# Two products with high and low values side by side, and probabilities scaled on another engine

## The chip, the cores and the metric

The kernel runs on one core of one Trainium2 chip. The metric is device time in microseconds (us) of one execution, the median of several runs. TensorE (PE in the profile) multiplies matrices, with weight loads shown as an engine of their own (PEld); VectorE is DVE, ScalarE is ACT, GpSimd is POOL, SyncE (SP) starts most DMA transfers. Each engine works through its own list of instructions strictly in order and waits at an instruction whose inputs or buffers are not ready.

## The reference, cut to what matters

One decoder layer over 1024 rows of width 1024: a token mixer, a cross-attention, a gated MLP. The change touches one head group of the mixer, sliding-window attention with 8 query heads that share 2 key and value heads of width 64, in blocks of 128 rows:

```
logits = einsum('bnqhgd,bnkhd->bnhgqk', qb, kb) * (SWA_HEAD_DIM ** -0.5)
logits = where(valid, logits + bias, -inf)
mx = maximum(logits.max(-1), sink)
p = exp(logits - mx)
probs = p / (p.sum(-1) + exp(sink - mx))
out = einsum('bnhgqk,bnkhd->bnqhgd', probs, vb)
```

Each block of 128 queries sees its own 128 keys and the 128 before them. Everything is in float32.

## The kernel before, in words

A float32 operand of a product is kept as two tiles, a rounded high part and the low part that is left (`hi_lo`: ScalarE copies, VectorE subtracts). A product is then three matmuls, `mm3`: high by high, high by low, low by high.

The mixer works through the sequence in two halves of 512 rows. In each half a generator, `swa`, walks through 16 items: 4 blocks of queries by 4 pairs of heads (`p`; its key and value head is `p // 2`). In the text items 0 to 15 are those of the first half, 16 to 31 those of the second. The generator hands its steps out between groups of matmuls of the projections, which are counted by an estimated clock (`tick`), so the place of each step in every engine's list is fixed when the program is built. Step *n* of `swa` issues, in this order: the logits of item *n* (`swa_logits`: four matmuls into a tile `lg`, then two custom VectorE instructions that write L and the row maxima `nm`), the values of item *n - 4* (`swa_values`, tile `pv`), the transposes of item *n - 2* (`swa_turn`, tile `tp`; ScalarE and VectorE make its two halves `pt`), the exponentials of item *n* (`swa_exp`, ScalarE, with the row sums `ssum`), and its scaling by the reciprocal of the sums (`swa_norm`). `lg`, `pv` and `tp` come from the pool `mx`, which has four PSUM banks; who gets which bank, and so who waits for whom, is decided when the program is built.

For most of items 1 to 11, and 17 to 27, the projections in between are the eight channel groups of `qk_proj`. Each has 24 matmuls of 512 columns, and a chain of its own (`qk_steps`): ScalarE copies the result (`xc`), GpSimd starts `cv`, VectorE adds three taps to `cv`, ScalarE takes a tanh (`th`), VectorE makes `qk` of it. In each group ScalarE and VectorE also split the weights that will be needed two groups on (`whi`, `wlo`).

`swv` holds the values: before, two tiles of 128 columns a block (both value heads), one with high and one with low parts. `swa_values` multiplies all 128 columns, though an item needs only the 64 of its own head:

```
mm3(pf, swv[0][:, cc, :], swv[1][:, cc, :], pt[0][:, m, :], pt[1][:, m, :], m == kb, m == 1)
r = slice(64 * (p // 2), 64 * (p // 2) + 64)
nc.scalar.copy(swT[h][p % 2][r, :, tt * P:(tt + 1) * P], pv[r])
```

`m` runs over the two blocks of keys; items 0 to 3 have one.

Of the kernel before, what the change touches and what calls it, by code (L numbers as in the profile page):

```python
# [7 lines left out]
F32 = mybir.dt.float32  # L8
F32R = mybir.dt.float32r
# [6 lines left out]
P = 128  # L16
# [12 lines left out]
def decoder_layer_kernel(ctx, tc, t, out):  # L29
    nc = tc.nc  # L30
    MUL, ADD, SUB, MAX, MIN = ALU.mult, ALU.add, ALU.subtract, ALU.max, ALU.min
# [47 lines left out]
    def hi_lo(hi, lo, src):  # L79
        nc.scalar.copy(hi, src)  # L80
        nc.vector.tensor_tensor(lo, in0=src, in1=hi.bitcast(F32), op=SUB)  # L81
# [63 lines left out]
    def mm3(ps, ahi, alo, bhi, blo, start, stop, more=False):  # L145
        nc.tensor.matmul(ps, lhsT=ahi, rhs=bhi, start=start, stop=False, skip_group_check=more)  # L146
        nc.tensor.matmul(ps, lhsT=ahi, rhs=blo, start=False, stop=False, skip_group_check=more)  # L147
        nc.tensor.matmul(ps, lhsT=alo, rhs=bhi, start=False, stop=stop, skip_group_check=more)  # L148
# [32 lines left out]
    def proj_tm(key, x, n, done, nt=4, before=None):  # L181
        pss = mm_tiles(nt)
        ws = {}
        us = 0.65 if n > 264 else 0.33
        a, b = range(0, nt // 2), range(nt // 2, nt)
        for j, tts in ((0, a), (1, a), (0, b), (1, b), (2, a), (2, b), (3, a), (3, b)):
            if before:
                before(j, tts is a)
            if j not in ws:
                ws[j] = weights(*key, j, ahead=2 if j != 1 else 0)  # L190
            elif (j, tts) == (1, b):
                stage(used[0] + 1)
            for tt in tts:
                for kk in range(2):
                    k, c = 2 * j + kk, slice(tt * P, (tt + 1) * P)
                    mm3(pss[tt][:, :n], x.hi(k, c), x.lo(k, c), ws[j][0][:, kk, :], ws[j][1][:, kk, :],
                        k == 0, k == KT - 1)
                    tick(us)
            if j == 3:
                for tt in tts:  # L200
                    done(tt, pss[tt])
# [65 lines left out]
    da = stA.enter_context(tc.tile_pool(name="da", bufs=1))  # L267
# [9 lines left out]

    kk = [da.tile([P, 5 * P], F32R, name=f"kk{i}") for i in range(2)]
    klo = [da.tile([P, 5 * P], F32R, name=f"klo{i}") for i in range(2)]
    swv = [da.tile([P, 5, P], F32R, name=f"swv{i}") for i in range(2)]  # L280
    halo = da.tile([P, 8, 3], F32, name="halo")
    gat = da.tile([P, 2, 4, 2, 16], F32, name="gat")
    mcol = da.tile([P, 3], F32, name="mcol")
# [4 lines left out]
    swT = [None, None]  # L288
# [40 lines left out]
    def ta_put(h, tt, ps):  # L329
        va = da.tile([P, 4, 129], F32, tag="va", name="va", bufs=5)  # L330
        nc.gpsimd.memset(va[:, :, 128:129], 1.0)
        va_t[4 * h + tt] = va
        nc.scalar.copy(va[:, 0, 0:128], ps[:, 0:128])
        hi_lo(swv[0][:, tt + 1, :], swv[1][:, tt + 1, :], ps[:, 128:256])
        for d in range(2):
            nc.vector.tensor_copy(gat[:, :, tt, d, 0:4], ps[:, 256:264].rearrange("p (a b) -> p a b", a=2))  # L336

    def tm_a(h, x):
        for z in swv:
            nc.vector.tensor_copy(z[:, 0, :], z[:, 4, :].bitcast(F32))  # L340
        proj_tm(("w_ta",), x, 264, lambda tt, ps: ta_put(h, tt, ps))

    def ta_first():
# [46 lines left out]
        for tt in range(4):  # L390
            ta_put(0, tt, pss[tt])
# [72 lines left out]
    def swa_norm(h, tt, p, kb, L, nm, sums):  # L464
        nc.vector.reciprocal(sums, sums)
        for b in range(2):
            Lv = L[:, b, kb * P:256]
            if b < 0:
                nc.scalar.mul(Lv, Lv, sums[:, b:b + 1])
            else:  # L470
                nc.vector.tensor_scalar(Lv, Lv, sums[:, b:b + 1], None, MUL)
        return h, tt, p, kb, L

    def swa_turn(h, tt, p, kb, L):
# [9 lines left out]
    def swa_values(h, tt, p, kb, pt):  # L484
        pv = mx.tile([P, 2, P], F32, tag="mx", name="pv")
        pf = pv.rearrange("p a b -> p (a b)")
        for m in range(kb, 2):
            cc = tt + m
            mm3(pf, swv[0][:, cc, :], swv[1][:, cc, :], pt[0][:, m, :], pt[1][:, m, :], m == kb, m == 1)
        r = slice(64 * (p // 2), 64 * (p // 2) + 64)  # L490
        nc.scalar.copy(swT[h][p % 2][r, :, tt * P:(tt + 1) * P], pv[r])

    def swa(h, swq, us):
        items = [(h, tt, p) for tt in range(4) for p in (0, 2, 1, 3)]
        lg, turned = [], []
        for n in range(len(items) + 4):
            if n < len(items):
                lg.append(swa_logits(*items[n], swq))
                yield 0.6
            if len(turned) == 2 or n == len(items) + 3:  # L500
                swa_values(*turned.pop(0))
                yield 0.6
            if n > 1 and lg:
                turned.append(swa_turn(*lg.pop(0)[:5]))
            if n >= len(items):
                yield us - 0.6
                continue
            yield 0.3
            swa_exp(*lg[-1])
            yield 0.65  # L510
            swa_norm(*lg[-1])
            yield us - (2.15 if n > 2 else 1.55)
# [224 lines left out]
    tm_o(1, x)  # L737
    drain()
    tm_a(1, x)
    also(gates(1, gt1, 2.7))  # L740
    s1 = also(swa(1, swq, 3.3), 1.0)
# [225 lines left out]
    vraw, graw, sums, pairs = {}, {}, {}, {}  # L967
# [281 lines left out]
    for h in range(2):  # L1249
# [5 lines left out]
        for tt in range(4):  # L1255
# [9 lines left out]
            if final:  # L1265
                for ch, b in ((1, 0), (0, None), (1, 1)):
                    v = slice(512 * ch, 512 * ch + 512) if b is None else slice(512 + 256 * b, 768 + 256 * b)
                    ps = banks[h, tt, ch][:, slice(0, 512) if b is None else slice(256 * b, 256 * b + 256)]
# [109 lines left out]
```

## Time and profile before

| | |
|---|---|
| median of 3 runs | 1415.21 us (1415.0 to 1415.45) |
| the profiled execution | 1416.47 us |
| its span, first to last instruction | 1414.8 us |
| PE busy | 1386.4 us, 98% |
| DVE busy | 973.1 us, 69% |
| ACT busy | 627.0 us, 44% |
| mean granted clock of TensorE | 0.995 |

The profile is of one execution, so its durations are set against 1416.47 us; 1.67 us of that lie outside the span. A busy share is a mean over the whole program: what bounds a stretch is read from the stretch.

### The profile page before, as it was taken

How to read it: one execution, taken by the hardware profiler on the slowest of the kernel's cores; microseconds unless marked ns; L12 is line 12 of the kernel's file. 1: busy time of each engine (PE TensorE's matmuls, PEld its weight loads, DVE VectorE, ACT ScalarE, POOL GpSimd, SP SyncE). 2: the span in 40 equal slices, each digit the busy share in tenths (PEclk: the TensorE clock that was granted, in tenths of full speed). 3: DMA queues.
4: the chain of work that ended last, by engine and by line, in shares of the span. 5: the costliest groups of instructions: out<-in, count | busy, mean ns of one | idle time of the engine just before them, and what ended most of it. 6: DMA issues, size and time to landing. Idle time of an engine off the chain costs nothing.

```text
span 1414.8 us, 18089 instructions
## 1 busy us (share of the span) xinstructions
PE 1386.4 (98%) x6866; PEld 1167.4 (83%) x6866; DVE 973.1 (69%) x1615; ACT 627.0 (44%) x1084; POOL 191.8 (14%) x256
## 2 busy tenths in 40 slices
PE   9999999999999999999987999999999999999997
PEld 7879888898888988888876788888888888888886
DVE  5687665996776676476585798777777877436525
ACT  6455434564253444334343454455445455323420
POOL 2231012321203010021071000000000000003002
PEclk9999999999999999999998999999999999999999
DMA  7314213124263321332133232222222238525821
GB/s 236 127 61 149 75 54 98 53 80 152 65 236 122 117 76 58 108 118 90 60 104 104 75 105 90 80 69 89 76 90 90 82 111 311 164 85 176 300 67 60
DMA packets 47575, 157.73 MB, mean 111 GB/s; under 512 B 5453, under 2 KB 6117, under 8 KB 46848
## 3 DMA queue, kind: packets, MB, share of 16 engines
q1 hardware_dynamic: 42912, 139.64, 30.7%
q0 software_dynamic: 4576, 16.94, 3.3%
q8 instruction: 54, 0.88, 0.3%
q14 instruction: 33, 0.27, 0.1%
HBM read 136.62 MB, written 21.51 MB: 112 GB/s over the span
## 4 chain that ended last, share of the span: by engine, by line
PE 86%; DVE 7%; ACT 3%; DMA 2%; issue 1%; SPq 0%; POOL 0%; DVEq 0%; ACTq 0%; POOLq 0%
PE upp L146 15%; PE upp L148 15%; PE upp L147 15%; PE ps L148 10%; PE ps L146 10%; PE ps L147 10%; DVE wlo L132 1%; PE tps L234 1%; PE tp L478 1%; ACT whi L131 1%; DVE cv L422 1%; DMA ud<-us 1%; DVE blk L916 1%; DMA selw<-in_sel 1%; DVE st L207 1%
## 5 line engine op out<-in xcount | busy, mean ns | idle before, releaser
L132 DVE TENSOR_TENSOR wlo<-raw,whi 128x1024 fp32r<-128x1024 f32 (+2 forms) x112 | 138.8, 1239 | 69.1 <-ACT whi L131 68.4
L148 PE MATMUL upp<-xc,blk 128*128 128x512 f32 x440 | 171.4, 390 | 1.3 <-DVE blk L916 1.3
L146 PE MATMUL upp<-xc,blk 128*128 128x512 f32 x440 | 171.4, 390 | 0.0
L147 PE MATMUL upp<-xc,blk 128*128 128x512 f32 x440 | 171.2, 389 | 0.0
L131 ACT CAST whi<-raw 128x1024 fp32r<-128x1024 f32 (+3 forms) x113 | 113.0, 1000 | 68.1 <-PE ps L148 46.2
L147 PE MATMUL upp<-dw,ag 128*128 128x512 f32 (+1 forms) x357 | 137.8, 386 | 0.0
L146 PE MATMUL upp<-dw,ag 128*128 128x512 f32 (+1 forms) x357 | 137.8, 386 | 0.0
L148 PE MATMUL upp<-dw,ag 128*128 128x512 f32 (+1 forms) x357 | 137.8, 386 | 0.0
L146 PE MATMUL ps<-aA,whi 128*128 128x512 f32 x336 | 134.9, 402 | 0.4 <-DVE gat L336 0.4
L148 PE MATMUL ps<-aA,wlo 128*128 128x512 f32 x336 | 131.6, 392 | 0.4 <-DVE wlo L132 0.4
L147 PE MATMUL ps<-aA,whi 128*128 128x512 f32 x336 | 131.3, 391 | 0.0
L1066 DVE SCALAR_TENSOR_TENSOR uc<-uc,fconv 128x1023 f32<-128x1023 f32 x88 | 112.8, 1282 | 26.7 <-ACT uc L1063 25.1
L148 PEld LDWEIGHTS upp<-xc,blk 128*128 128x128 f32 x440 | 82.6, 188 | 19.2 <-DVE blk L916 1.9
L146 PEld LDWEIGHTS upp<-xc,blk 128*128 128x128 f32 x440 | 82.6, 188 | 17.3 <-issue 0.3
L147 PEld LDWEIGHTS upp<-xc,blk 128*128 128x128 f32 x440 | 82.6, 188 | 17.1
L146 PE MATMUL ps<-whi,aA 128*128 128x512 f32 (+2 forms) x256 | 92.4, 361 | 1.2 <-ACT aA L80 1.2
L148 PE MATMUL ps<-whi,aA 128*128 128x512 f32 (+2 forms) x256 | 90.0, 352 | 0.2 <-DVE aA L81 0.2
L147 PE MATMUL ps<-wlo,aA 128*128 128x512 f32 (+2 forms) x256 | 89.7, 350 | 0.0
L1057 DVE TENSOR_TENSOR uc<-upp,uc 128x512 f32<-128x512 f32 x66 | 45.4, 688 | 59.3 <-PE upp L148 54.5
L81 DVE TENSOR_TENSOR ag<-araw,ag 128x512 fp32r<-128x512 f32 x44 | 31.0, 705 | 73.4 <-ACT ag L80 73.4
L146 PE MATMUL upp<-aA,blk 128*128 128x512 f32 x176 | 70.9, 403 | 10.0 <-DVE uc L1057 10.0
L147 PEld LDWEIGHTS upp<-dw,ag 128*128 128x128 f32 x357 | 67.0, 188 | 13.7
(405 smaller groups left out, 3165.5 us busy)
## 6 DMA issues: line engine op xcount, KB each, us to landing
raw<-in_w_up SPq DMA_DIRECT2D x48, 512.0 KB, 3.6
raw<-in_w_down SPq DMA_DIRECT2D x44, 512.0 KB, 4.5
raw<-in_w_cm SPq DMA_DIRECT2D x26, 512.0 KB, 3.7
ad<-uc POOLq DMA_DIRECT2D x22, 512.0 KB, 3.6
araw<-ad SPq DMA_DIRECT2D x44, 256.0 KB, 4.8
raw<-in_w_out SPq DMA_DIRECT2D x16, 512.0 KB, 5.1
raw<-in_wq SPq DMA_DIRECT2D x16, 512.0 KB, 3.6
raw<-in_wo SPq DMA_DIRECT2D x16, 512.0 KB, 3.6
```

The source lines that it names most:

```text
L81: nc.vector.tensor_tensor(lo, in0=src, in1=hi.bitcast(F32), op=SUB)
L131: nc.scalar.copy(hi[:, c], raw[:, c])
L132: nc.vector.tensor_tensor(lo, in0=raw, in1=hi.bitcast(F32), op=SUB)
L146: nc.tensor.matmul(ps, lhsT=ahi, rhs=bhi, start=start, stop=False, skip_group_check=more)
L147: nc.tensor.matmul(ps, lhsT=ahi, rhs=blo, start=False, stop=False, skip_group_check=more)
L148: nc.tensor.matmul(ps, lhsT=alo, rhs=bhi, start=False, stop=stop, skip_group_check=more)
L207: nc.vector.bn_stats(st[:, i, :], y[:, i * 512:(i + 1) * 512])
L234: nc.tensor.transpose(ps[:, k * P:(k + 1) * P], y[:, kk * P:(kk + 1) * P], ident)
L422: nc.vector.scalar_tensor_tensor(cv, in0=xc[:, j:j + 512], scalar=mlc[:, i, j:j + 1], in1=cv, op0=MUL, op1=ADD)
L478: nc.tensor.transpose(tp[:, m, b, :], L[:, b, m * P:(m + 1) * P], ident)
L1057: nc.vector.tensor_tensor(dst, in0=ps, in1=y, op=ADD)
L1066: nc.vector.scalar_tensor_tensor(u[:, d:S], in0=x[:, 0:S - d], scalar=fconv[:, i, 2 - d:3 - d], in1=u[:, d:S], op0=MUL, op1=ADD)
```

## The change

The high and low columns of one value head now lie side by side, 64 and 64, in one tile `swv` (the second head has them the other way round). One matmul with these 128 columns as weights gives the product of the high values in one half of the partitions and that of the low values in the other. Two such matmuls a block, one with the high and one with the low part of the probabilities, take the place of three. The two halves of `pv` must then be added: ScalarE copies the low half to its place in `swT`, and VectorE adds the high half onto it. The product of the two low parts, which was left out before, is now part of the result. And the scaling of the probabilities in `swa_norm` moves from VectorE to ScalarE.

```
-    swv = [da.tile([P, 5, P], F32R, name=f"swv{i}") for i in range(2)]
+    swv = da.tile([P, 5, 4, 64], F32R, name="swv")
...
-        hi_lo(swv[0][:, tt + 1, :], swv[1][:, tt + 1, :], ps[:, 128:256])
+        hi_lo(swv[:, tt + 1, 0::3, :], swv[:, tt + 1, 1:3, :], ps[:, 128:256].rearrange("p (a b) -> p a b", a=2))
...
-        for z in swv:
-            nc.vector.tensor_copy(z[:, 0, :], z[:, 4, :].bitcast(F32))
+        nc.vector.tensor_copy(swv[:, 0], swv[:, 4].bitcast(F32))
...
-            if b < 0:
-                nc.scalar.mul(Lv, Lv, sums[:, b:b + 1])
-            else:
-                nc.vector.tensor_scalar(Lv, Lv, sums[:, b:b + 1], None, MUL)
+            nc.scalar.mul(Lv, Lv, sums[:, b:b + 1])
...
+        kv = p // 2
         for m in range(kb, 2):
-            cc = tt + m
-            mm3(pf, swv[0][:, cc, :], swv[1][:, cc, :], pt[0][:, m, :], pt[1][:, m, :], m == kb, m == 1)
-        r = slice(64 * (p // 2), 64 * (p // 2) + 64)
-        nc.scalar.copy(swT[h][p % 2][r, :, tt * P:(tt + 1) * P], pv[r])
+            w = swv[:, tt + m, 2 * kv:2 * kv + 2, :].rearrange("p a b -> p (a b)")
+            for i in range(2):
+                nc.tensor.matmul(pf, lhsT=w, rhs=pt[i][:, m, :], start=m == kb and i == 0, stop=m == i == 1)
+
+        r, o = slice(64 * kv, 64 * kv + 64), slice(64 - 64 * kv, 128 - 64 * kv)
+        dst = swT[h][p % 2][r, :, tt * P:(tt + 1) * P]
+        nc.scalar.copy(dst, pv[o])
+        nc.vector.tensor_tensor(dst, in0=pv[r], in1=dst, op=ADD)
```

On ScalarE, in the second half, from the exponentials of item 23, the list before is this (L, ssum and nm are the logits, sums and maxima of an item; xc, th and whi belong to the channel groups):

```order
L462 ACTIVATE L,ssum<-L,nm 128x257 x2
L426 ACTIVATE th<-cv 128x512
L414 COPY xc<-ps 128x512
L131 CAST whi<-raw 128x768
L491 COPY swT<-pv 64x2x128
L80 CAST pt<-tp 128x512
```

and this now:

```order
L461 ACTIVATE L,ssum<-L,nm 128x257 x2
L467 ACTIVATE L<-L,ssum 128x256 x2
L425 ACTIVATE th<-cv 128x512
L413 COPY xc<-ps 128x512
L131 CAST whi<-raw 128x768
L491 COPY swT<-pv 64x2x128
L80 CAST pt<-tp 128x512
```

The two scalings (L467) stand between the exponentials, whose sums VectorE must first invert, and everything else of ScalarE.

On VectorE, at the same place, before (the two ISA rows with L are the maxima of an item):

```order
L465 RECIPROCAL ssum<-ssum 128x2
L471 TENSOR_SCALAR L<-L,ssum 128x256 x2
L428 SCALAR_TENSOR_TENSOR qk<-th,cv 128x512
L132 TENSOR_TENSOR wlo<-raw,whi 128x768
L454 ISA L,nm<-lg,btab,nsnk 128x256
L454 ISA nm 128x1
L454 ISA L,nm<-lg,btab,nsnk 128x256
L454 ISA nm 128x1
L422 SCALAR_TENSOR_TENSOR cv<-xc,mlc,cv 128x512
```

and now:

```order
L464 RECIPROCAL ssum<-ssum 128x2
L427 SCALAR_TENSOR_TENSOR qk<-th,cv 128x512
L132 TENSOR_TENSOR wlo<-raw,whi 128x768
L453 ISA L,nm<-lg,btab,nsnk 128x256
L453 ISA nm 128x1
L453 ISA L,nm<-lg,btab,nsnk 128x256
L453 ISA nm 128x1
L492 TENSOR_TENSOR swT<-pv,swT 64x2x128
L421 SCALAR_TENSOR_TENSOR cv<-xc,mlc,cv 128x512
```

The scalings have gone from between the reciprocal and `qk`, and the addition (L492) comes in behind the maxima, before the next tap.

On PE, in the first half, the logits of an item and the values behind them, with the engines whose semaphores each waits for, before:

```order
L446 MATMUL lg<-kk_105,swq 128x256 [waits DVE_49]
...
L146 MATMUL pv<-pt,swv_109 128x256 [waits Activation_49]
L147 MATMUL pv<-pt,swv_109 128x256
L148 MATMUL pv<-pt,swv_110 128x256
...
L478 MATMUL tp<-ident,L 128x128 [waits DVE_49]
```

and now:

```order
L445 MATMUL lg<-kk_105,swq 128x256 [waits DVE_49]
...
L487 MATMUL pv<-pt,swv 128x256 [waits DVE_49,Activation_49]
L487 MATMUL pv<-pt,swv 128x256 x3
...
L474 MATMUL tp<-ident,L 128x128 [waits DVE_49]
```

The banks are dealt out otherwise. Before, `pv` took the bank of the `pv` of the step before and waited for its copy on ScalarE, and `tp` waited for the maxima of the step before. Now `pv` takes the bank of the `lg` of the step before and waits for those maxima on VectorE, and `tp` takes the bank of the `pv` of the step before and waits for its addition.

## Rows read from the trace of the kernel before

**Rows 1.** The page: busy time of PE, and the chain that ended last.

```profile
PE 1386.4 (98%) x6866; PEld 1167.4 (83%) x6866; DVE 973.1 (69%) x1615; ACT 627.0 (44%) x1084; POOL 191.8 (14%) x256
PE 86%; DVE 7%; ACT 3%; DMA 2%; issue 1%; SPq 0%; POOL 0%; DVEq 0%; ACTq 0%; POOLq 0%
```

**Rows 2.** Busy time in stretches (start:end, length, then each engine's, with instructions).

```profile
60.00:80.00 20.00, 18.62 (x97) 15.18 (x96) 16.29 (x47) 10.67 (x31) 7.16 (x12) 1.00 0.34 97
100.00:120.00 20.00, 20.00 (x128) 18.95 (x127) 19.53 (x52) 12.96 (x33) 6.04 (x11) 1.00 0.24 72
260.00:280.00 20.00, 18.36 (x105) 15.63 (x104) 19.17 (x45) 11.62 (x29) 6.22 (x10) 1.00 0.20 62
```

**Rows 3.** What PE waited for, 40 to 130 and 240 to 352 us: total, times, longest.

```profile
PE tp L478 <- DVE nm L454: 1.9, 3, 1.1
...
PE tp L478 <- DVE nm L454: 1.6, 1, 1.6
```

**Rows 4.** Groups of instructions by line and form: busy us, mean ns | idle before.

```profile
L147 PE MATMUL pv<-pt,swv 128*128 128x256 f32 x60 | 16.9, 282 | 0.0
L471 DVE TENSOR_SCALAR L<-L,ssum 128x256 f32<-128x256 f32 x56 | 17.6, 356 | 1.0
L462 ACT ACTIVATE L<-L,nm 128x257 f32<-128x257 f32 x56 | 28.1, 505 | 18.6 <-DVE nm L454 16.7 <-POOL L L449 1.8
L80 ACT CAST aA<-xraw 128x256 fp32r<-128x256 f32 x2 | 0.7, 400 | 0.0
L81 DVE TENSOR_TENSOR pt<-tp,pt 128x256 fp32r<-128x256 f32 x4 | 1.7, 414 | 0.0
```

**Rows 5.** PE in order of time: values of item 8, logits of items 21 and 25.

```profile
116.46 0.28 PE L146 MATMUL pv<-pt,swv 128*128 128x256 f32 x1
...
117.16 0.34 PE L146 MATMUL ps<-whi,aA 128*128 128x384 f32 x1
...
266.34 0.28 PE L446 MATMUL lg<-kk,swq 128*128 128x256 f32 x1
...
289.41 0.28 PE L446 MATMUL lg<-kk,swq 128*128 128x256 f32 x1
...
311.02 0.28 PE L146 MATMUL pv<-pt,swv 128*128 128x256 f32 x1
```

**Rows 6.** VectorE in order of time, between the reciprocals of items 20 and 24.

```profile
270.92 0.16 DVE L465 RECIPROCAL ssum<-ssum 128x2 f32<-128x2 f32 x1
271.12 0.62 DVE L471 TENSOR_SCALAR L<-L,ssum 128x256 f32<-128x256 f32 x2
271.65 0.48 DVE L454 CUSTOM_DVE_ANT_0 L<-lg,btab,nsnk 128x256 f32<-128x256 f32 x1
...
273.71 1.37 DVE L132 TENSOR_TENSOR wlo<-raw,whi 128x1024 fp32r<-128x1024 f32 x1 [0.57 <-ACT whi L131]
...
281.68 1.23 DVE L132 TENSOR_TENSOR wlo<-raw,whi 128x1024 fp32r<-128x1024 f32 x1 [1.15 <-ACT whi L131]
...
288.52 0.96 DVE L132 TENSOR_TENSOR wlo<-raw,whi 128x768 fp32r<-128x768 f32 x1
...
292.92 0.16 DVE L465 RECIPROCAL ssum<-ssum 128x2 f32<-128x2 f32 x1
```

**Rows 7.** ScalarE in order of time, behind the reciprocal of item 20.

```profile
271.10 0.63 ACT L426 ACTIVATE th<-cv 128x512 f32<-128x512 f32 x1 [1.68 <-DVE ssum L465]
271.76 0.37 ACT L491 COPY swT<-pv 64x256 f32<-64x256 f32 x1
272.15 0.59 ACT L414 COPY xc<-ps 128x512 f32<-128x512 f32 x1
272.63 1.05 ACT L131 CAST whi<-raw 128x1024 fp32r<-128x1024 f32 x1
```

**Rows 8.** VectorE: the last reading of the maxima of items 11 and 28.

```profile
117.15 0.08 DVE L454 DVE_READ_ACCUMULATOR2_ANT nm<- 128x1 f32 x1
...
310.60 0.08 DVE L454 DVE_READ_ACCUMULATOR2_ANT nm<- 128x1 f32 x1
```

## The prediction

> **What bounds the kernel now.** I read the page first: PE is busy 98% of the span and holds 86% of the chain that ended last [rows 1]. So a matmul that goes away is a gain, unless PE then waits for something else. Next I read busy time by stretch, in the two places where the sliding-window items run. Around 100 to 120 us VectorE is busy 19.53 of 20 us, and at 260 to 280 it is busy 19.17 while PE has 1.6 us without work; at 60 to 80 PE has 1.4 us without work. ScalarE has 11 to 13 of 20 [rows 2]. The list of PE's waits names what it stood still for: the transposes `tp`, held by the row maxima of VectorE, 1.9 us in the first half and 1.6 in the second [rows 3]. So in these stretches two things run neck and neck: PE's own list, and a loop of VectorE and ScalarE that hands PE its banks and operands. The question is not what PE saves but what the loop does.
>
> The pace of each can be read. From the logits of item 21 to those of item 25 PE takes 289.41 - 266.34 = 23.07 us [rows 5]. Over the same four items and three channel groups VectorE takes 292.92 - 270.92 = 22.0 us between two reciprocals at the same place of the pattern [rows 6]. The loop has 1 us to spare in four items, no more.
>
> **PE: two matmuls for three.** The six value matmuls of an item go from 116.46 to 117.16, 0.117 us each from start to start (the 282 ns of a row overlap with the next) [rows 4, 5]. There are 60 of each of the three kinds [rows 4], so 60 go away: 60 x 0.117 = 7.0 us, 0.234 an item with two blocks. The whole of it counts only where PE sets the pace. In the four items above PE would need 23.07 - 0.94 = 22.1 us.
>
> **VectorE: scalings out, additions in.** A pair of scalings moves the next instruction from 271.12 to 271.65, 0.53 us [rows 6]; four items give 2.1. An addition of 64 x 256 from PSUM is not in the trace; the nearest row is the subtraction into `pt` of 256 columns, 414 ns [rows 4], some 0.35 from start to start if neighbours overlap as those above do. Four cost 1.4 us. A half or the double of this moves the four items by 0.7 or 1.4 us. If nothing new waited, the loop would be at 22.0 - 2.1 + 1.4 = 21.3 us.
>
> **ScalarE: what the scaling is queued in front of.** The trace has no scaling there. Two rows bound it: a CAST of 128x256 from SBUF to SBUF, 400 ns, and the exponential of 128x257, 505 ns, which also has per-partition operands and a sum to give [rows 4]. Less the 0.09 us by which neighbours overlap (the tanh of 0.63 us and the copy behind it show no more), that is 0.31 to 0.41 us each, 0.62 to 0.82 a pair. ScalarE has room for it by busy time; its order is the trouble. The pair waits for the reciprocal, and behind it stand the tanh `th`, which VectorE's `qk` waits for, then `xc`, `whi`, for which `wlo` waits, and the copy into `swT`, for which the addition waits. Today `th` starts at 271.10, as soon as the reciprocal is out, and VectorE scales meanwhile [rows 6, 7]: the two overlap. After the change they are in series.
>
> I lay the three channel groups out by these rows, with 0.41 for a scaling. First group: after the reciprocal VectorE does the maxima (0.81) and then the addition, which needs pair 0.8, `th` 0.55, `swT` 0.37 on ScalarE: it waits 0.9. `whi` ends 3.2 us after the reciprocal (`xc` 0.48 and `whi` 1.05 behind that); `wlo` waits 0.5, where it waits 0.57 today. Second group: the scaling stands behind `whi` in the list, and `wlo` waits 0.95, today 1.15. Third group: `qk` directly behind the reciprocal waits for pair and tanh, 0.8 + 0.63 = 1.45, and `wlo` for `xc` and `whi` 0.6; today none of both. In sum 4.4 us of waiting where there is 1.7 now [rows 6], 2.7 more: the loop takes 21.3 + 2.7 = 24.0 us, and with 0.31 for a scaling 23.6 (the pair counts in two of the groups). That is 1.6 to 2.0 us more than now, 0.4 to 0.5 an item, and more than the 22.1 that PE would need. So in the channel groups the loop sets the pace and PE's saving is lost there.
>
> The rule that speaks against this edit has a page: the Trainium skill, "ScalarE: Activation LUTs", section "Rules for kernel authors", sends multiplications to VectorE and not to ScalarE. Its section "What ACT_TABLE_LOAD costs" gives 186 ns plus 0.833 ns an element, 93 more for a per-partition operand and 93 of overlap, so as an estimate 0.40 us for a scaling here, and a sum at the upper end below. No run shows it yet; the 505 ns agree with it as far as they go.
>
> **Who waits for the loop.** As the lists show, the values of a step now wait for the maxima of the step before; it was the transposes, 1.2 us later in PE's list, that did. So the bound on how far VectorE may lag has become tighter.
>
> First half: from item 1 to item 11 the loop loses ten times 0.4 to 0.5, 4 to 5 us, and the maxima of item 11 end at 121.2 to 122.2 where they end at 117.23 [rows 8]. The values of item 8, in the step after, stand at 116.46 [rows 5] and must wait for them: 4.8 to 5.8 us late. Behind them the channel groups are over, VectorE has less to do, PE sets the pace and eight items save 0.234 each, 1.9. The first half: +2.9 to +3.9 us.
>
> Second half: items 16 to 19 lose the scalings (2.1 us of VectorE) and have no addition yet, since values come four steps later, and PE's wait of 1.6 us lies there. Between 0 and 2.1 I take 1.2 as the gain. Then seven items lose 2.8 to 3.5, so the maxima of item 28 end 1.6 to 2.3 us late, at 312.3 to 313.0 [rows 8]; the values of item 25 stand at 311.02 [rows 5] and are 1.3 to 2.0 late. Seven items behind save 1.6: -0.3 to +0.4 us.
>
> The rest of the change costs nothing that can be read: the split of the values writes the same elements, one copy of 256 columns stands for two of 128 once, and the later program is bound by PE and only starts earlier or later.
>
> **The sum** is +2.6 to +4.3 us. I take the lower end, since the CAST is nearer in kind to a scaling than the exponential with its sum: 1416.47 + 2.6 = 1419.1 us for a profiled execution, which stood 1.26 above the median of before, so 1417.8 us as a median.
>
> **Rivals.** *PE's saving arrives.* For it: 98% PE, ScalarE idle a third of the time, VectorE relieved by 2.1 - 1.4. The halves add up to 17 x the loss per item, less 4.3 us of everything else; so the sum is negative as soon as the loop loses less than 0.25 us an item, 1.0 in four, instead of 1.6 to 2.0. That needs most of the two waits of the third group to fall into time in which VectorE would have waited anyway. At no loss it gives -4.3 us, 1410.9; with PE bound throughout -7.0, and the 3.5 us of [rows 3] at most on top, 1408.2 to 1404.7. Against it: VectorE is full there, so a wait of its is not free.
>
> *The addition is the wait* (slower). It holds its bank, for which the next transposes wait, and VectorE's whole list stands behind it. In my layout it waits 0.9 us in one item of four. If ScalarE is behind at every item, it waits in the other three as well: up to 0.9 x 13 = 11.5 us, half of it likelier, +8, 1423. It decides where the copy into `swT` ends later than the maxima ahead of the addition. Today the copy of item 17 is done at 272.13, at the same time as the maxima of item 21 [rows 6, 7], with no margin once ScalarE gets later.
>
> *It does nothing:* the two pull even; that is the upper part of the first rival and the lower part of the forecast, not a case of its own.
>
> **How the numbers follow.** About 2.8 us, 0.2%, is what a measurement can tell from no change. The forecast, loop-bound with 0.3 to 0.5 us an item and the addition somewhere between, has 0.62 and its own range 1414.5 to 1420.5; 0.36 of it is within 0.2%, 0.26 above. The saving arrives: 0.27, of which 0.25 is faster by more than 0.2%. The addition waits: 0.11, all slower. So faster 0.25, same 0.38, slower 0.37. The range 1410.5 to 1421.5 leaves out half of the first rival and about half of the second, some 0.19.
>
> **What the profile of the changed kernel would show.** PE: 120 value matmuls in place of 180. ScalarE: 64 scalings of 0.4 to 0.5 us, and idle time ahead of them ended by the reciprocal. VectorE: `qk` waiting for `th`, and `swT` for ScalarE, some 1 to 1.5 us each time; the four items between the reciprocals of items 20 and 24 at 23.6 to 24 us. PE: waits at `pv`, ended by the maxima. I would be wrong if those four items take under 23 us, if PE waits less than before in both halves, or if the scalings are not what `th` waits for.

## The result, and the profile after

The changed kernel takes **1427.88 us** (median of 4 runs, 1424.66 to 1431.08), the kernel before 1415.33: a ratio of 1.0091, with a 95% interval of 1.0076 to 1.0106. It is slower by 12.6 us, where 1417.8 was forecast and 1421.5 was the end of the range. The profiled execution has a span of 1427.7 us.

The page: busy time, and the chain of work that ended last [rows 1 for before].

```profile
PE 1385.5 (97%) x6806; PEld 1162.8 (81%) x6806; DVE 968.8 (68%) x1582; ACT 655.1 (46%) x1148; POOL 188.3 (13%) x256
PE 78%; DVE 11%; ACT 6%; DMA 2%; issue 2%; POOL 0%; SPq 0%; DVEq 0%; ACTq 0%; POOLq 0%
```

PE has the 60 matmuls less that the change takes away, but its share of the chain fell from 86 to 78%, and what it lost went to VectorE and ScalarE. Its busy time alone hides this: 1385.5 us against 1386.4. (In e9 below, with the same matmuls and fewer waits, it is 1379.4.)

Busy time by stretch (columns as in [rows 2]; the last stretch is new):

```profile
60.00:80.00 20.00, 17.67 (x89) 13.93 (x88) 14.73 (x36) 12.98 (x36) 5.76 (x12) 1.00 0.30 94
100.00:120.00 20.00, 18.46 (x106) 15.91 (x104) 16.39 (x36) 13.38 (x33) 5.20 (x11) 1.00 0.23 67
260.00:280.00 20.00, 17.96 (x97) 14.84 (x96) 16.16 (x33) 13.30 (x32) 6.83 (x12) 1.00 0.15 46
318.00:343.00 25.00, 20.44 (x129) 18.53 (x129) 16.52 (x38) 20.68 (x50) 0.76 (x2) 1.00 0.27 83
```

In the kernel before, the work of that last stretch lies some 8 us earlier:

```profile
310.00:335.00 25.00, 24.98 (x165) 23.32 (x164) 20.43 (x49) 18.52 (x45) 1.01 (x3) 1.00 0.28 85
```

At 100 to 120 us PE was full and VectorE was busy 19.53 us. Now both have holes, 1.5 us and 3.6 us, and ScalarE is not full either. No engine is the bound; they wait for each other. The last stretch lies behind the channel groups, where the prediction saw PE alone setting the pace: PE has 4.6 us of 25 without work, and before it had none.

What PE waited for from 50 to 365 us (total, times, longest) [rows 3]:

```profile
PE pv L487 <- DVE nm L453: 10.5, 10, 1.9
PE wps L588 <- DVE swT L492: 1.6, 1, 1.6
PE pv L487 <- DVE pt L81: 1.3, 1, 1.3
PE tp L474 <- ACT th L425: 1.2, 1, 1.2
PE tps L234 <- DVE aA L81: 1.2, 1, 1.2
```

Before there were four waits of `tp`, 3.5 us. Now the values `pv` wait ten times for the maxima, 10.5 us, and others that were not there come on top. The groups by form (busy, mean ns | idle before) [rows 4]:

```profile
L467 ACT ACTIVATE L<-L,ssum 128x256 f32<-128x256 f32 x56 | 25.5, 503 | 33.1 <-DVE ssum L464 33.1
L487 PE MATMUL pv<-pt,swv 128*128 128x256 f32 x120 | 20.5, 290 | 12.6 <-DVE nm L453 10.5 <-DVE pt L81 1.3 <-ACT pt L80 0.8
L492 DVE TENSOR_TENSOR swT<-pv,swT 64x256 f32<-64x256 f32 x32 | 13.4, 420 | 12.1 <-ACT swT L491 11.8
L491 ACT COPY swT<-pv 64x256 f32<-64x256 f32 x32 | 11.8, 368 | 10.6 <-PE pv L487 10.0
```

Two waits face each other here: ScalarE stands 33.1 us ahead of the scalings of full width until VectorE's reciprocal is out, and VectorE stands 11.8 us ahead of the additions until ScalarE's copy is out.

In order of time, VectorE and then ScalarE in the steps of items 28 and 29, behind the channel groups:

```profile
319.90 0.96 DVE L132 TENSOR_TENSOR wlo<-raw,whi 128x768 fp32r<-128x768 f32 x1 [0.62 <-ACT whi L131]
320.78 0.16 DVE L464 RECIPROCAL ssum<-ssum 128x2 f32<-128x2 f32 x1
...
322.37 0.43 DVE L492 TENSOR_TENSOR swT<-pv,swT 64x256 f32<-64x256 f32 x1 [0.64 <-ACT swT L491]
323.44 1.22 DVE L132 TENSOR_TENSOR wlo<-raw,whi 128x1024 fp32r<-128x1024 f32 x1 [0.64 <-ACT whi L131]
...
325.90 0.15 DVE L464 RECIPROCAL ssum<-ssum 128x2 f32<-128x2 f32 x1
327.50 0.69 DVE L81 TENSOR_TENSOR aA<-tps,aA 128x512 fp32r<-128x512 f32 x1 [1.45 <-ACT aA L80]
```

```profile
321.03 0.92 ACT L467 ACTIVATE L<-L,ssum 128x256 f32<-128x256 f32 x2 [1.16 <-DVE ssum L464]
321.97 0.37 ACT L491 COPY swT<-pv 64x256 f32<-64x256 f32 x1
322.36 1.05 ACT L131 CAST whi<-raw 128x1024 fp32r<-128x1024 f32 x1
323.31 0.58 ACT L80 CAST pt<-tp 128x512 fp32r<-128x512 f32 x1
...
324.27 0.52 ACT L461 ACTIVATE L<-L,nm 128x257 f32<-128x257 f32 x1
...
326.09 0.91 ACT L467 ACTIVATE L<-L,ssum 128x256 f32<-128x256 f32 x2 [0.72 <-DVE ssum L464]
326.90 0.57 ACT L80 CAST aA<-tps 128x512 fp32r<-128x512 f32 x1
```

Read them as one chain. ScalarE stands 1.16 us for the reciprocal, scales, and only then copies `swT` and casts `whi`; VectorE stands 0.64 us for each of the two. The next reciprocal stands behind VectorE's `wlo`, and ScalarE stands 0.72 us for it; it scales, and only then casts `aA`, for which VectorE stands 1.45 us. The two engines take turns in waiting for each other.

Where each kernel lost its time is read from the start of the value matmuls of some items, in us of the profiled executions (e1 to e10 are below). The values of the items up to 8 and from 16 to 24 run beside the channel groups, the others behind them.

| item | before | after | e1 | e2 | e3 | e6 | e9 | e10 |
|---|---|---|---|---|---|---|---|---|
| 0 | 71.8 | 71.2 | 71.0 | 70.6 | 73.1 | 70.6 | 70.1 | 70.7 |
| 8 | 116.5 | 121.2 | 119.3 | 116.7 | 117.0 | 116.2 | 113.4 | 112.1 |
| 9 | 121.2 | 127.3 | 124.0 | 121.6 | 121.7 | 120.8 | 118.9 | 116.6 |
| 15 | 150.5 | 155.1 | 151.7 | 150.7 | 149.4 | 149.2 | 146.7 | 144.4 |
| 23 | 301.5 | 307.8 | 303.2 | 300.8 | 299.4 | 298.8 | 296.0 | 293.6 |
| 25 | 311.0 | 318.5 | 313.4 | 311.3 | 309.5 | 309.2 | 306.0 | 302.6 |
| 31 | 348.4 | 361.3 | 351.5 | 352.1 | 347.1 | 349.8 | 342.9 | 339.6 |

After the last of these items the two kernels keep their distance: 12.9 us there, and 12.9 us between the spans of the two profiled executions (between the medians it is 12.6). Of the 12.9, 4.7 were lost up to item 15, 1.6 more up to item 23, and 6.6 in the last eight items.

### The profile page after: what moved, and what is told of

It reads as the page before. It is cut to its first block, busy times and chain, and to the rows that moved or that the text cites. A ratio compares the mean times of both kernels' runs of the same rounds, so it can differ in the third digit from the quotient of the medians.

```text
span 1427.7 us, 17990 instructions
## 1 busy us (share of the span) xinstructions
PE 1385.5 (97%) x6806; PEld 1162.8 (81%) x6806; DVE 968.8 (68%) x1582; ACT 655.1 (46%) x1148; POOL 188.3 (13%) x256
## 4 chain that ended last, share of the span: by engine, by line
PE 78%; DVE 11%; ACT 6%; DMA 2%; issue 2%; POOL 0%; SPq 0%; DVEq 0%; ACTq 0%; POOLq 0%
PE upp L146 15%; PE upp L148 15%; PE upp L147 15%; PE ps L146 9%; PE ps L148 9%; PE ps L147 9%; DVE cv L421 2%; DVE wlo L132 2%; ACT whi L131 1%; DVE L L453 1%; ACT L L467 1%; PE tps L234 1%; DVE blk L917 1%; ACT L L461 1%; DVE y L227 1%
## 5 line engine op out<-in xcount | busy, mean ns | idle before, releaser
L132 DVE TENSOR_TENSOR wlo<-raw,whi 128x1024 fp32r<-128x1024 f32 (+2 forms) x112 | 139.1, 1242 | 71.3 <-ACT whi L131 70.1
```

The source lines that it names most:

```text
L132: nc.vector.tensor_tensor(lo, in0=raw, in1=hi.bitcast(F32), op=SUB)
```

## The experiments

Two theories went in. The first: the scaling on ScalarE, directly behind the reciprocal and ahead of what others wait for, is the cause. The rival: the addition on VectorE and its wait are the cause. Ratios are to the kernel before, timed on the same chip, with 95% intervals; a difference of two such ratios is uncertain by some 0.13 to 0.20%, 2 to 3 us.

**One part at a time.** e1 is the change with the scaling put back, e2 the kernel before with the scaling alone moved:

```
# e1: after with
nc.vector.tensor_scalar(Lv, Lv, sums[:, b:b + 1], None, MUL)
# e2: before with
nc.scalar.mul(Lv, Lv, sums[:, b:b + 1])
```

> The changed kernel with the scaling of the probabilities put back on VectorE; the two products and the addition stay. If the scaling on ScalarE is the cause (queued behind the reciprocal and ahead of the copies that TensorE waits for), the loss of 12.6 us goes, and the two products' saving, up to 7.0 us, begins to show: 1411 to 1417 us. If the addition on VectorE and the wait of the values' products for the maxima of the step before are the cause, it stays at 1423 to 1428. If it is the sheer number of instructions on VectorE, which gets the scalings back on top of the additions, it is 1428 to 1434.

> The kernel before with nothing changed but the scaling, which ScalarE does; three products as before, no addition. If the scaling on ScalarE is the cause, nearly the whole loss is here, and without the saving of the products: 1424 to 1435 us. If the addition is the cause, VectorE has lost work and gained none, and the time is 1411 to 1417.

Measured: e1 1417.48 us, 1.0021 [1.0012, 1.0029]; e2 1418.71 us, 1.0030 [1.0019, 1.0042]. Either part alone costs 3 to 4 us, both together 12.9. Neither theory holds alone. By the table e2 is 0.7 us ahead of before at item 23 and 3.7 behind at item 31: all of its loss lies in the last eight items, where the prediction saw a gain.

**The same scaling, one step later.** e3 takes the scalings of the changed kernel out of the place behind the reciprocal; e8 does the same in the kernel before.

```
 def swa_norm(...): nc.vector.reciprocal(sums, sums)      # scalings taken out
+def swa_scale(...): the two nc.scalar.mul
 in swa, step n:
+            swa_scale(*lg[-2])      # of step n-1, ahead of the exponentials of step n
             swa_exp(*lg[-1])
```

> The changed kernel with the scalings on ScalarE still, but written one step later, ahead of the next step's exponentials, so that they no longer stand directly behind the reciprocal for which they wait. If ScalarE's standing still for the reciprocal is what the scaling costs, most of the loss goes: 1414 to 1420 us. If the 0.4 to 0.5 us that each scaling occupies ScalarE is what costs, wherever it stands, it remains at 1422 to 1428. If the addition is the cause, 1426 to 1429.

> The kernel before with the scalings on ScalarE, written one step late; three products and no addition. VectorE is rid of the scalings. If ScalarE's standing still behind the reciprocal is the whole cost of the moved scaling (4.4 us in the run that moved it alone), this is 1412 to 1416 us, at the time of the kernel before or a little below, since VectorE has less to do. If the 0.4 to 0.5 us of each scaling on ScalarE cost by themselves, 1417 to 1420.

Measured: e3 1414.04 us, 0.9997 [0.9988, 1.0006]; e8 1413.36 us, 0.9995 [0.9986, 1.0003]. The whole loss is gone, with the same 64 scalings on ScalarE and the same additions on VectorE. What ScalarE waited for in e3 (us, times), in the first row ahead of the exponentials, in the second ahead of the scalings:

```profile
  DVE nm L453: 5.5, 5
  DVE ssum L464: 2.8, 5
```

In the changed kernel these are 9.4 us in 9 times, and 37.8 us in 32 with the narrow scalings counted in. So not the 0.4 us of a scaling cost the time, but its place in the list: 35 us more in which ScalarE stood still for the reciprocal, with `swT`, `whi`, `aA` and the next exponentials behind it.

**The addition, taken off VectorE or off its wait.** e4 adds on GpSimd with the scaling on VectorE; e5 on GpSimd with the late scaling; e12 on GpSimd with the scaling as changed; e7 on VectorE, but from two copies (scaling on VectorE); e11 is the change with the addition moved behind the subtraction.

```
# e4, e5, e12 (e7: nc.vector in the last line)
nc.scalar.copy(dst, pv[r])
nc.scalar.copy(low_[r], pv[o])
nc.gpsimd.tensor_tensor(dst, in0=dst, in1=low_[r], op=ADD)
# e11: in swa, behind swa_turn
nc.vector.tensor_tensor(dst, in0=pv[r], in1=dst, op=ADD)
```

> Two products, the scaling on VectorE, and the addition taken off VectorE: ScalarE copies both row groups out of the bank and GpSimd adds them. VectorE then does what it did before the change. If the scaling on ScalarE is the whole cause, this is like the run with the scaling alone put back, within 2 us, 1410 to 1417. If the addition on VectorE is the cause or a part of it, this is below that run by 3 us or more, and the products' saving shows: 1408 to 1412. If ScalarE's second copy and GpSimd's addition make the next step's values late, it is 1416 to 1424.

> Two products; the scalings on ScalarE, written one step late as in the run that did that alone (1414.0 us); and the addition on GpSimd, ScalarE copying both row groups out. VectorE is rid of both the scalings and the additions. If what is left of the loss in the run with late scaling is VectorE's 0.35 us per addition, TensorE is the bound nearly everywhere and most of the 7.0 us of products shows: 1407 to 1411 us. If the loss that is left comes from ScalarE, which now does two scalings, two casts and two copies an item, the time stays at 1413 to 1418.

> Two products, the scaling on VectorE, and the addition on VectorE too, but from two copies that ScalarE makes, so that ScalarE's copies free the bank and no bank waits for VectorE's queue. Against the run with the scaling put back (1417.5 us): if that run loses because the bank is held until VectorE has come to the addition, this is 1412 to 1416. If it loses by the time of the additions on VectorE, it stays at 1416 to 1420, and against the run with the addition on GpSimd (1416.2) it tells what VectorE's additions cost.

> The changed kernel, scaling on ScalarE directly behind the reciprocal, with one line moved: the addition is written behind the subtraction of the transposed probabilities, so that ScalarE's copy of the other row group, which stood queued behind the scalings, has ended by then. In the changed kernel VectorE waited 11.8 us in 12 places for that copy. If this wait, VectorE for a copy that is queued behind scalings that wait for VectorE's reciprocal, is what the two parts of the change cost together over what they cost alone, the time falls to 1418 to 1422 us. If it is the 0.35 us of each addition on VectorE, it stays at 1425 to 1429.

> The changed kernel, scaling on ScalarE directly behind the reciprocal, with the addition on GpSimd (ScalarE copies both row groups out). VectorE neither adds nor waits for ScalarE's copy. If the wait or the additions on VectorE made up the 9 us between the changed kernel and the run without an addition (1418.9), this is 1418 to 1422 us. If ScalarE's queue alone is the cause, which has one copy more an item here, it is 1425 to 1430.

| run | scaling | addition | us | ratio |
|---|---|---|---|---|
| e4 | VectorE | GpSimd | 1416.19 | 1.0015 [1.0006, 1.0024] |
| e5 | ScalarE, late | GpSimd | 1413.78 | 0.9995 [0.9987, 1.0004] |
| e7 | VectorE | VectorE, from copies | 1417.01 | 1.0018 [1.0009, 1.0027] |
| e11 | ScalarE | VectorE, behind `pt` | 1430.77 | 1.0116 [1.0103, 1.0129] |
| e12 | ScalarE | GpSimd | 1427.48 | 1.0094 [1.0081, 1.0107] |

e11 is the one that tells most. It did what it was made for: the wait of `swT` for ScalarE's copy fell from 11.8 us in 12 places to one of 0.6. The time did not fall; it rose. VectorE's wait for the cast of `pt` grew from 2.2 to 7.8 us (7.9 in the kernel before), and PE stood for the subtraction behind it:

```profile
PE tp L474 <- DVE pt L81: 7.7, 6, 2.3
PE pv L487 <- DVE nm L453: 4.3, 4, 1.7
```

So taking the addition's wait away gives nothing back: the wait showed that ScalarE was late. That speaks against the rival's mechanism, though the rival's time (1423) was nearer than the forecast. By itself e11 does not refute it, since the addition holds its bank longer there. e12 has the same loss with no addition on VectorE at all, but it brings in a copy and GpSimd's addition, which cost as much (below). What bounds the rival are runs with no addition on any engine: from e9 to e6, below, the scaling alone costs 0.58%, 8.2 us. With the addition on VectorE, from e1 to the changed kernel, it costs 0.70%, 9.9 us. The 1.7 us between the two, uncertain by some 3, are what the addition and its wait add to the price of the scaling.

The other dealing of the banks is not what makes the scaling dear: e2 and e6 are dealt as before the change, with `tp` waiting for the maxima and `pv` for ScalarE's copies, and the scaling costs 4.2 and 8.2 us there. With the scaling on VectorE the dealing costs nothing that can be measured: in e7 the copies free the bank early, the banks are dealt as before, and the time is within 0.03% of e1, with one copy more (0.9 us by e14, below). Beside the scaling behind the reciprocal it was not tried by itself.

GpSimd's addition is no free one either. With the late scaling (e5) it gains nothing measurable over VectorE's (e3), and e4 is 0.32%, 4.5 us, slower than the same kernel with the copy and no addition (e14, below). In e4, VectorE's two scalings take 1.14 us where they take 0.62 [rows 6], while GpSimd adds:

```profile
119.00 1.14 DVE L467 TENSOR_SCALAR L<-L,ssum 128x256 f32<-128x256 f32 x2
```

```profile
119.26 0.73 POOL L494 TENSOR_TENSOR swT<-swT,vlo 64x256 f32<-64x256 f32 x1 [3.99 <-ACT vlo L493]
```

The Trainium skill, "GPSIMD Engine Reference", section "Key points", says that GpSimd shares its SBUF interfaces with VectorE, with "contention with DVE instructions in a 2-port perf mode or with two SBUF inputs". The two rows agree that there is contention; no run here shows whether the scaling is such an instruction.

**Without an addition.** e6 (scaling as changed), e9 (on VectorE) and e10 (on ScalarE, late) have two products and one copy alone, now of the half with the values' high parts:

```
-nc.scalar.copy(dst, pv[o])
-nc.vector.tensor_tensor(dst, in0=pv[r], in1=dst, op=ADD)
+nc.scalar.copy(dst, pv[r])
```

> The changed kernel without the addition: ScalarE copies the row group with the probabilities' product with the values' high parts, and the product with their low parts is left out of the output. Scaling on ScalarE directly behind the reciprocal, as in the change. The scaling moved alone cost 4.4 us. If the two parts of the change only add up, this is that run with the products' saving, 1411 to 1416 us. If the scaling on ScalarE is by itself what costs 12 us once the products are short, it is 1423 to 1428.

> The products' saving by itself: two products, the scaling on VectorE as in the kernel before, and no addition, so that the product with the values' low parts is left out of the output. VectorE and ScalarE do what they do in the kernel before; only TensorE has less, 7.0 us. If TensorE sets the pace nearly everywhere here, 1407 to 1410 us. If VectorE stands so close behind it that the time saved turns into waiting for VectorE, 1411 to 1415. The run with the addition on VectorE took 1417.5, and the difference to it is the price of the addition where the scaling stays on VectorE.

> Two products, the scalings on ScalarE one step late, and no addition (the product with the values' low parts is left out of the output). VectorE has 2.1 us per four items less to do than before the change, TensorE 0.94. If VectorE was what took the products' saving, TensorE is the bound here: 1405 to 1409 us. If ScalarE with its late scalings is the next bound, it stays at 1412 to 1415, as in the three runs with late scalings so far.

Measured: e6 1418.91 us, 1.0035 [1.0023, 1.0046]; e9 1410.87 us, 0.9977 [0.9968, 0.9987]; e10 1408.05 us, 0.9960 [0.9947, 0.9972]. This prices the products and the addition (0.1% is 1.4 us):

| scaling | products, three to two | then the addition on VectorE |
|---|---|---|
| VectorE | -0.23%, -3.3 us | e9 to e1: +0.44%, +6.2 us |
| ScalarE, behind the reciprocal | e2 to e6: +0.05%, +0.7 us | e6 to after: +0.56%, +7.9 us |
| ScalarE, late | e8 to e10: -0.35%, -4.9 us | e10 to e3: +0.37%, +5.2 us |

Of the 7.0 us that PE saves, 3.3 arrive where VectorE still scales, 4.9 with the late scaling, and nothing that can be measured where the scaling stands behind the reciprocal. And the addition costs at least what the products bring in every row; in the last one the two cannot be told apart. In e10 PE is nearly the only bound; all its waits from 50 to 365 us are

```profile
PE kps L599 <- DVE pt L81: 1.1, 1, 1.1
PE tp L475 <- ACT L L469: 1.0, 2, 0.7
```

**An idle copy.** If VectorE and ScalarE work in turns, any instruction on either lengthens the round. e13 is e6, e14 is e9, each with a copy on ScalarE that nothing reads:

```
 nc.scalar.copy(dst, pv[r])
+nc.scalar.copy(low_[r], pv[o])
```

> The run without an addition (scaling on ScalarE directly behind the reciprocal, 1418.9 us; the product with the values' low parts is left out of the output) with one thing more: ScalarE copies the other row group out too, and nothing reads it. If VectorE and ScalarE work in turns here, each waiting for the other, so that any instruction on either lengthens the round, the copy's 0.35 us an item cost nearly what the addition on VectorE cost, 8 us: 1424 to 1428. If only VectorE's time or GpSimd's addition counts, it stays at 1418 to 1420.

> The same idle copy beside the run of two products alone with the scaling on VectorE (1410.9 us; the product with the values' low parts is left out). ScalarE has idle time there. If the round between the two engines exists only with the scaling behind the reciprocal, the copy is free: 1410 to 1412. If it costs here too, it is 1414 to 1417, and the 5.4 us that the addition on GpSimd cost were ScalarE's copy and not GpSimd's.

Measured: e13 1422.78 us, 1.0064 [1.0051, 1.0077]; e14 1412.48 us, 0.9983 [0.9973, 0.9993]. The same copy costs 0.29%, 4.1 us, with the scaling behind the reciprocal, and 0.06%, 0.9 us and not to be told from nothing, with the scaling on VectorE. The round in turns is there, but the copy costs about half of what was forecast for it. It also divides e12: of its 8.3 us over e6 the copy is half and GpSimd's addition the other, 4.2 us.

**Half as many additions.** e15 (late scaling) and e16 (scaling on VectorE) add for two items at once, 128 partitions in place of 64:

```
-nc.scalar.copy(dst, pv[o])
-nc.vector.tensor_tensor(dst, in0=pv[r], in1=dst, op=ADD)
+nc.scalar.copy(dst, pv[r])
+nc.scalar.copy(half[0][r], pv[o])      # one tile for the items of both kv
 # behind swa_turn of every second item:
+nc.vector.tensor_tensor(pair[0], in0=pair[0], in1=pair[1], op=ADD)
```

> The whole computation: two products, scalings on ScalarE one step late, and one addition for two items: ScalarE copies both row groups of both items out, and VectorE adds 128 partitions at once, 16 additions in place of 32, behind the subtraction of the transposed probabilities. If the price of the addition is the number of VectorE's instructions, half of the 6 us between 1408.0 and 1414.0 comes back: 1410 to 1412 us, below the kernel before. If ScalarE's second copy costs as much, 1413 to 1417.

> The whole computation: two products, scaling on VectorE as in the kernel before, and the addition by pairs of items as in the run beside it, 16 additions on VectorE and two copies an item on ScalarE. By the number of VectorE's instructions, half of the 6.2 us between 1410.9 and 1417.5: 1413 to 1415 us. If ScalarE's copies cost, or the late addition holds something up, 1416 to 1419.

Measured: e15 1412.81 us, 0.9993 [0.9984, 1.0002]; e16 1414.58 us, 1.0002 [0.9993, 1.0010]. e16 gets 2.3 us back against e7, which has the same copies and 32 additions. That fits a price in VectorE's time, though the additions of e16 also stand at another place of the list. For e15 against e3 the 0.6 us are within the uncertainty. No kernel that computes the whole is measurably faster than the one before.

## Why the prediction was wrong, step by step

- **PE: two matmuls for three.** Right in count (120) and in size: PE is busy 1379.4 us in e9 and 1386.4 before, 7.0 less. In time 4.9 of them arrive where little else waits (e8 to e10).
- **The scaling's and the addition's durations.** 0.31 to 0.41 us were given for a scaling; the row says 503 ns, a pair 0.91, so 0.41 from start to start. The upper end was right, and I had chosen the lower. The estimate by the Trainium skill, "ScalarE: Activation LUTs", section "What ACT_TABLE_LOAD costs", was 0.40; the trace agrees. The addition takes 420 ns, forecast from a row of 414.
- **ScalarE: the queue, and the loop at 23.6 to 24.0 us.** Right in mechanism and, beside the channel groups, nearly in size. The reciprocals of items 5 and 9 lie 24.0 us apart (21.7 before), those of items 20 and 24 24.6 us (22.0 before). Between the latter two the layout had five waits of VectorE, 0.9, 0.5, 0.95, 1.45 and 0.6, in sum 4.4 us. The trace has these five, 4.6 us (the last is put down to PE):

```profile
276.96 0.43 DVE L492 TENSOR_TENSOR swT<-pv,swT 64x256 f32<-64x256 f32 x1 [1.09 <-ACT swT L491]
278.51 1.53 DVE L132 TENSOR_TENSOR wlo<-raw,whi 128x1024 fp32r<-128x1024 f32 x1 [0.41 <-ACT whi L131]
286.42 1.23 DVE L132 TENSOR_TENSOR wlo<-raw,whi 128x1024 fp32r<-128x1024 f32 x1 [1.09 <-ACT whi L131]
293.38 0.69 DVE L427 SCALAR_TENSOR_TENSOR qk<-th,cv 128x512 f32<-128x512 f32 x1 [1.50 <-ACT th L425]
294.58 1.16 DVE L132 TENSOR_TENSOR wlo<-raw,whi 128x768 fp32r<-128x768 f32 x1 [0.51 <-PE lg L446]
```

- **Who waits.** Right: `pv` for the maxima, and item 8 came 4.7 us late where 4.8 to 5.8 were given. That the tighter bound costs anything by itself is not seen: e7, dealt as before, is as slow as e1.
- **What failed: "Behind them the channel groups are over, VectorE has less to do, PE sets the pace", and for the second half "Seven items behind save 1.6".** These items were priced with PE alone, and the loop of VectorE and ScalarE at nothing. In the second half the loop sets the pace there too: from item 25 to item 31 the forecast had -1.6 us and the trace has +5.4 (item 25 is 7.5 us late, item 31 12.9). The same serial order of reciprocal, scaling and what is queued behind it holds there, with other work in it (`whi`, `wlo`, the casts of `aA`). e2 shows it with one edit: it loses 3.5 us in this stretch, and e6 against e9 3.7, without any addition. Even e9, with the scaling on VectorE, gains only 0.5 us there. About 1.6 of the 5.4 us go to TensorE's clock (last section). In the first half the clause itself held: behind item 8 PE has no wait over 0.2 us, and from item 9 to item 15 the kernel makes up 1.4 us, 0.24 an item. What took the forecast's 1.9 us there is one step: from item 8 to item 9 the lag grows from 4.7 to 6.1 us, with no wait and the clock at the lower level. The forecast laid ScalarE's list out for three channel groups and not for the steps behind them. Of the 10.3 us between forecast and trace (+2.6 and +12.9), 7.0 lie in the second half's stretch and 1.9 in the first half's.
- **A size that was off: the seven items of the second half.** They were given 2.8 to 3.5 us less a gain of 1.2 at the start. The loop was 2.6 us longer in four items and not 1.6 to 2.0, and the values of item 25 came 3.1 us later than the logits of item 16 had been, not 1.3 to 2.0. That is 1.8 us of the 10.3.
- **The addition as a term.** 1.4 us in four items was its time on VectorE, and beside the channel groups that was right: the distances of 24.0 and 24.6 us between the reciprocals are 22.7 and 23.0 in e6, which has no addition. Behind the channel groups nothing was charged for it. Over the whole kernel it costs 5.2 to 7.9 us in 32 items (table above).
- **The rival of the addition's wait.** It put up to 11.5 us of waiting on the addition, beside the channel groups; 11.8 were there, but the nearness is luck. Beside the channel groups it is 4.4 us in four places, one item of four, as in the forecast's own layout. Of the rest 5.4 us lie between 124 and 152 us, where PE waits for nothing. And e11 took nearly all of it away and gained nothing. What was forecast as a cause is in the main a symptom. (The copy of item 17 also had some margin before the change: the maxima of item 21 are two instructions, of which [rows 6] shows the first, and end at 272.5 us, not 272.13.)

The sum along one path of runs: products -3.3 (e9), addition +6.2 (e1), scaling on ScalarE behind the reciprocal +9.9 (after); 12.8 us, of 12.9 by the ratio. Along the other: scaling +4.2 (e2), products +0.7 (e6), addition +7.9. Both sums close by construction; what they show is that a price depends on what else is there. The scaling costs 4 us beside three products and 8 to 10 beside two. That the third product covers a part of it is the likely reason, and not shown by itself.

**What stays open.** That the place of the scaling is the main cause, and not its time on ScalarE, is shown by e3 and e8. With it put right the change still gains nothing, since the addition takes what the products bring. Which of the instructions queued behind it (`swT`, `whi`, `aA`, the exponentials) costs how much was not tried one by one. Why e11 is slower than the change by 0.25% was not followed up either; the bank that the addition holds longer is a guess.

## What to carry to other kernels

An instruction that moves to an idle engine takes its wait along: what counts is not the 0.4 us that it occupies there but who is queued behind it while it waits. Write it where its operand has long been ready; one step later made the same move free here (ratio 1.0091 to 0.9997). And when an edit lengthens a round between two engines, lay their lists out for every stretch in which the round runs, also where a third engine seemed to set the pace; a wait in the list is a cause only when taking it away gives the time back.

## What was not expected of the hardware

TensorE's clock fell after some of the waits. After the wait of 1.86 us ahead of item 8's values (121.16 us), and again at the waits of 1.55 and 0.49 us at 342.58 and 343.57, the granted clock falls to 0.50, the lower of the two levels, and comes back after 3.4 us (PEclk is the first number behind the busy times):

```profile
120.00:122.00 2.00, 0.84 (x5) 0.87 (x6) 1.94 (x7) 1.98 (x7) 0.00 (x0) 0.91 0.14 55
122.00:124.00 2.00, 2.00 (x9) 1.91 (x9) 1.66 (x7) 1.24 (x5) 0.09 (x1) 0.50 0.01 4
124.00:126.00 2.00, 2.00 (x11) 2.00 (x10) 1.44 (x3) 1.98 (x6) 0.10 (x1) 0.74 0.03 8
...
344.00:346.00 2.00, 2.00 (x8) 1.71 (x7) 1.67 (x5) 0.03 (x1) 0.23 (x1) 0.50 0.00 0
```

Twelve matmuls of 384 columns start over 2.73 us there, from 123.43 to 126.16; at the full clock, in the same kernel, they take 2.01 (115.57 to 117.58). What the two falls cost can be read, since PE waits for nothing during them. From the values of item 8 to those of item 9 it takes 6.18 us, where it took 4.76 before and the third product's 0.23 are gone: 1.65 us. From the transposes `kps` at 343.57 to the values of item 29 at 346.99 it takes 3.42 us, where it took 1.84 before: 1.58. So about 3.2 of the 12.9 us of this execution are the clock. A wait can cost its own length and something after it, but need not: after the waits of 1.71 us at 85.70 and 1.74 us at 272.11 the granted clock stays at 1.00. The four executions of the changed kernel spread from 1424.66 to 1431.08 us, those of before from 1415.0 to 1416.38; whether the clock makes this spread is not shown. It is not the main cause: e12, as slow as the change, has a granted clock of 1.00 in both stretches.

```profile
50.00:155.00 105.00, 97.74 (x517) 81.54 (x518) 69.55 (x152) 76.28 (x185) 30.91 (x53) 1.00 0.30 96
240.00:365.00 125.00, 115.19 (x656) 98.24 (x655) 87.70 (x210) 89.09 (x216) 34.02 (x58) 1.00 0.29 95
```
